# A dilated 3x3 convolution: two weight kinds of pairs 3 to 6 as 128-row matmuls over a doubled copy of the odd rows

## The chip, the cores and the metric

The kernel runs on one core of a Trainium2 chip. The metric is device time in microseconds (us) of one execution. Three runs of the kernel before gave 126.81, 126.86 and 127.06 us; the median is 126.86 us. One further execution was profiled; everything said about single instructions and transfers comes from that one.

Engines are named as in the profile: PE is TensorE (PEld is its loading of weights), DVE is VectorE, ACT is ScalarE, POOL is GpSimd, and SP is SyncE, whose queue issues all transfers of this kernel.

## The reference

A batch of 16 images with 64 channels of 64 x 64 is convolved to 128 channels with a 3 x 3 kernel of dilation 2 and zero padding, in float32:

```python
batch, c_in, h, w, c_out, k, dilation = 16, 64, 64, 64, 128, 3, 2
pad = dilated_k // 2                       # 2
for kh in range(k):
    for kw in range(k):
        output[b, co] += weight[co, ci, kh, kw] * x_pad[b, ci, kh*dilation:kh*dilation+h, kw*dilation:kw*dilation+w]
```

So an output row r needs the input rows r-2, r and r+2, each at three column shifts. 16.8 MB are read and 33.6 MB are written.

## The kernel before

**Layout.** Two images make a pair: the 64 channels of the one lie on partitions 0 to 63, those of the other on 64 to 127. There are 8 pairs (0 to 7), and each is cut into 4 groups of 16 output rows, so there are 32 groups G; `pb, g = divmod(G, 4)` gives the pair and the group in it.

**Arithmetic.** The rows are taken two by two. In each block of four rows, rows 0 and 1 are the even part E and rows 2 and 3 the odd part O. Dilation 2 means that the row above an even part is the odd part of the block before, and the row below it is the odd part of its own block. With w0, w1, w2 for the three kernel rows, the kernel forms E+O once and then

- even output = w1 (E+O) + (w2-w1) O + w0 O of the block before,
- odd output = w1 (E+O) + (w0-w1) E + w2 E of the block after.

The five products are called kinds 0 to 4: w1, w2-w1, w0, w0-w1, w2. `product` (line 182) makes one kind: for each of three column shifts j, and for each of the two images, one matmul that contracts over 64 partitions (the two halves of the array work on the two images) with up to 512 columns. `psP` (kind 0, 6 matmuls), `psA` (kinds 1 and 2, 12 matmuls, even output) and `psB` (kinds 3 and 4, 12 matmuls, odd output) are PSUM tiles of two banks; psP has one buffer, psA and psB share three.

**One group** (lines 219 to 263): PE makes psP, psA, psB in this order (in G = 0: psA, psB, psP). ACT copies psP to `p_sb` (L251), then does its casts. DVE makes the sum E+O of the next group (`rowsum`, L95), then adds psA + p_sb and psB + p_sb into the output ring `osb` (L258), a ring of three pairs.

**Casts.** x arrives as float32 (`x32`, three buffers) and is cast to float16 (`x16`, four buffers) in chunks of a group, at the places of the hand-written table `CASTS` (L162): ACT (L83) or POOL (L85). POOL has 7 of the 32 chunks, the last at G = 6.

**Transfers.** All are issued by SP in program order, which is the order of the one queue: the weights; pair 0 in two pieces, pairs 1 and 2; then, by the table `LOADS` (L215), pair 3 in G = 0, 4 in G = 2, 5 in G = 3, 6 in G = 7, 7 in G = 11. A load waits until the casts of the pair that had its buffer are done. A pair's output goes out when its last group is added (`pair_store`, two transfers of 2 MB); the first four rows of one image go out at G = 0. Pair 7 goes out in halves: at G = 29 one image's 32 rows (1 MB), the other's first 24 rows (768 KB) and its next `ROWS4` = 8 rows as two transfers, partitions 0 to 123 (248 KB) and 124 to 127 (8 KB); at G = 31 two transfers of 1 MB.

**Opening.** The weights are combined on DVE, POOL and ACT, turned by matmuls against an identity and copied into `w_sb`, duplicated on both halves of the partitions (lines 113 to 158).

Of the kernel before, what the change touches and what calls it, by code (L numbers as in the profile page):

```python
# [10 lines left out]
def kernel(  # L11
# [7 lines left out]
    nc = tc.nc  # L19

    B, CI, H, W = x.shape
    CO, CI_w, KH, KW = weight.shape
# [4 lines left out]
    d = 2  # L27

    P = 128
    f32 = mybir.dt.float32  # L30
    f16 = mybir.dt.float16
# [5 lines left out]
    NG = H // GR  # L37
    NBLK = GR // 4
    NH = GR // 2 * W
    npairs = B // 2  # L40
    ngroups = npairs * NG
# [3 lines left out]

    wpool = ctx.enter_context(tc.tile_pool(name="wpool", bufs=1))
    fpool = ctx.enter_context(tc.tile_pool(name="fpool", bufs=XF))
    xpool = ctx.enter_context(tc.tile_pool(name="xpool", bufs=4))
    sxpool = ctx.enter_context(tc.tile_pool(name="sxpool", bufs=2))
    opool = ctx.enter_context(tc.tile_pool(name="opool", bufs=1))  # L50
    spool = ctx.enter_context(tc.tile_pool(name="spool", bufs=3))
# [1 line left out]
    apool = ctx.enter_context(tc.tile_pool(name="apool", bufs=3, space=bass.MemoryType.PSUM))  # L53
# [6 lines left out]
    x32_tiles, x16_tiles, xs_tiles = {}, {}, {}  # L60

    def load(pb, cuts=(0, H)):
        x32_tiles[pb] = fpool.tile([P, HW], f32, tag="x32", name="x32")
        for lo, hi in zip(cuts[:-1], cuts[1:]):
            nc.sync.dma_start(
                out=x32_tiles[pb][:, lo * W : hi * W], in_=x_pair[pb, :, lo * W : hi * W]
            )
# [3 lines left out]
    def o_pair(pb):  # L71
        at = pb % OB * 2 * HW
        return o_ring[:, at : at + 2 * HW]

    def cast(c, eng):
        pb, g = divmod(c, NG)
        lo, hi = chunk_rows[g]
        if g == 0:
            x16_tiles[pb] = xpool.tile([P, HW], f16, tag="x16", name="x16")
        out = x16_tiles[pb][:, lo * W : hi * W]  # L80
        in_ = x32_tiles[pb][:, lo * W : hi * W]
        if eng is nc.scalar:
            eng.copy(out=out, in_=in_)  # L83
        else:
            eng.tensor_copy(out=out, in_=in_)  # L85

    def rowsum(c):
        pb, g = divmod(c, NG)
        if g == 0:
            xs_tiles[pb] = sxpool.tile([P, HW // 2], f16, tag="xs", name="xs")  # L90
        v = x16_tiles[pb][:, g * GR * W : (g + 1) * GR * W].rearrange(
            "p (b e q) -> p b e q", e=2, q=2 * W
        )
        s = xs_tiles[pb][:, g * NH : (g + 1) * NH].rearrange("p (b q) -> p b q", q=2 * W)
        nc.vector.tensor_tensor(out=s, in0=v[:, :, 0], in1=v[:, :, 1], op=add)  # L95

    w32 = wpool.tile([CO, CI * KH * KW], f32, name="w32")
    nc.sync.dma_start(out=w32, in_=weight.rearrange("o i h w -> o (i h w)"))
    load(0, (0, 2 * GR + d, H))
# [1 line left out]
    load(2)  # L101
    zero = wpool.tile([P, 512], f16, name="zero")
    nc.vector.memset(zero, 0.0)  # L103
    ident = wpool.tile([P, P], f16, name="ident")
    make_identity(nc, ident)

# [11 lines left out]
    w_sb = wpool.tile([P, NT * CO], f16, name="w_sb")  # L118
# [10 lines left out]
    def turn(k):  # L129
# [24 lines left out]
        out=x16_tiles[0][:, 8 * W : 18 * W], in_=x32_tiles[0][:, 8 * W : 18 * W]  # L154
# [5 lines left out]

    A, B_ = nc.scalar, nc.gpsimd
    CASTS = {  # L162
        0: ((1, A), (2, A), (3, B_)),
        1: ((4, A), (5, A), (6, B_)),
        2: ((7, A), (8, A), (9, B_)),
        3: ((10, A), (11, B_)),
        4: ((12, A), (13, A), (14, B_)),
        5: ((15, A), (16, B_)),
        6: ((17, A), (18, A), (19, B_)),
        8: ((20, A), (21, A)),  # L170
        9: ((22, A), (23, A)),
        19: ((24, A), (25, A)),
        20: ((26, A), (27, A)),
        24: ((28, A), (29, A)),
        25: ((30, A), (31, A)),
    }

    def casts(G):
        for c, eng in CASTS.get(G, ()):
            cast(c, eng)  # L180

    def product(ps, src, kind, blk0, nblk, first, last):
        for j in (1, 0, 2):
            dw = (j - 1) * d
            o0, o1 = max(0, -dw), W - max(0, dw)
            t = kind * KW + j
            for hb in range(2):
                pp = slice(hb * CI, (hb + 1) * CI)
                rhs = src(pp, dw + o0, dw + o1)
                po = ps[:, hb * NH + blk0 * 2 * W : hb * NH + (blk0 + nblk) * 2 * W]  # L190
                po = po.rearrange("p (r w) -> p r w", w=W)[:, :, o0:o1]
                nc.tensor.matmul(  # L192
                    out=po,
                    lhsT=w_sb[pp, t * CO : (t + 1) * CO],
                    rhs=rhs,
                    start=first and j == 1,
                    stop=last and j == 2,
                )

    def blocks(x16, b0, n, e):  # L200
        v = x16.rearrange("p (b e r w) -> p b e r w", e=2, r=2, w=W)
        return lambda pp, c0, c1: v[pp, b0 : b0 + n, e, :, c0:c1]

    def store(pb, m, r0=0, r1=H, rows=((0, P),)):
        for lo, hi in rows:
            nc.sync.dma_start(
                out=out_img[2 * pb + m, lo:hi, r0 * W : r1 * W],
                in_=o_pair(pb)[lo:hi, m * HW + r0 * W : m * HW + r1 * W],
            )

    def pair_store(pb):
        for m in range(2):
            store(pb, m, GR // 4 if pb == m == 0 else 0)

    LOADS = {0: (3,), 2: (4,), 3: (5,), 7: (6,), 11: (7,)}  # L215
    FOUR = ((0, P - 4), (P - 4, P))
    ROWS4 = 8

    for G in range(ngroups):
        pb, g = divmod(G, NG)  # L220
        x16 = x16_tiles[pb]
        xs = xs_tiles[pb].rearrange("p (r w) -> p r w", w=W)
        o = o_pair(pb).rearrange("p (m b e q) -> p m b e q", m=2, e=2, q=2 * W)
        b0 = g * NBLK

        def summed():
            ps = ppool.tile([P, 2 * NH], f32, tag="p", name="psP")
            sv = lambda pp, c0, c1: xs[pp, g * GR // 2 : (g + 1) * GR // 2, c0:c1]
            product(ps, sv, 0, 0, NBLK, True, True)
            return ps  # L230

        if G:
            psP = summed()

        psA = apool.tile([P, 2 * NH], f32, tag="ab", name="psA")
        product(psA, blocks(x16, b0, NBLK, 1), 1, 0, NBLK, True, False)
        z = 1 if g == 0 else 0
        product(psA, blocks(x16, b0 + z - 1, NBLK - z, 1), 2, z, NBLK - z, False, True)

        psB = apool.tile([P, 2 * NH], f32, tag="ab", name="psB")  # L240
        product(psB, blocks(x16, b0, NBLK, 0), 3, 0, NBLK, True, False)
        z = 1 if g == NG - 1 else 0
        product(psB, blocks(x16, b0 + 1, NBLK - z, 0), 4, 0, NBLK - z, False, True)

        if not G:
            psP = summed()

        if not G:
            casts(0)
        p_sb = spool.tile([P, 2 * NH], f32, tag="psb", name="p_sb")  # L250
        nc.scalar.copy(out=p_sb, in_=psP)  # L251
        if G:
            casts(G)
        if G + 1 < ngroups:
            rowsum(G + 1)
        pv = p_sb.rearrange("p (m b q) -> p m b q", m=2, q=2 * W)
        for e, ps in ((0, psA), (1, psB)):
            nc.vector.tensor_tensor(  # L258
                out=o[:, :, b0 : b0 + NBLK, e],
                in0=ps.rearrange("p (m b q) -> p m b q", m=2, q=2 * W),  # L260
                in1=pv,
                op=add,
            )

        later = pb in (1, 2)
        if g == NG - 1 and later:
            pair_store(pb)
        for q in LOADS.get(G, ()):
            load(q)
        if G == 0:  # L270
            store(0, 0, 0, GR // 4)
        if pb == npairs - 1:
            if g % 2 == 1:
                store(pb, 0, (g - 1) * GR, (g + 1) * GR)
                if g == 1:
                    store(pb, 1, 0, 2 * GR - ROWS4)
                    store(pb, 1, 2 * GR - ROWS4, 2 * GR, FOUR)
                else:
                    store(pb, 1, (g - 1) * GR, (g + 1) * GR)
        elif g == NG - 1 and not later:  # L280
            pair_store(pb)
# [35 lines left out]
```

## Time and profile before

| | |
|---|---|
| median of three runs | 126.86 us (126.81 to 127.06) |
| the profiled execution: its own time | 126.71 us |
| its span, first to last instruction | 124.9 us |
| PE busy | 104.9 us, 84% |
| DVE busy | 92.1 us, 74% |
| ACT busy | 58.7 us, 47% |
| POOL busy | 9.6 us, 8% |
| transfers | 50.78 MB, 405 GB/s of HBM traffic over the span |
| one psA or psB matmul of 64 x 496 | 369 ns from start to modelled end |
| one p_sb copy | 1012 ns |
| one add into osb | 1224 ns (psA), 1220 ns (psB) |
| one rowsum | 468 ns mean, 416 ns median |

A busy time is the union of an engine's instructions. The page's second part cuts the span into 40 slices (3.12 us each) and gives busy tenths; its chain of work starts at the instruction that ended last and goes back to what released each step. Matmuls overlap, so a matmul's 369 ns is longer than the step from one to the next. A transfer is spread over 16 DMA engines, and each engine reports by itself when its part has landed; the trace keeps these reports and each packet's start and length.

### The profile page before, as it was taken

Reading aid. Unit: us, or ns where it says so; the run is one execution under the profiler, and the core shown is the slowest. Engines: PE = TensorE matmul, PEld = TensorE weight load, DVE = VectorE, ACT = ScalarE, POOL = GpSimd, SP = SyncE. Lnnn points to the kernel's source line nnn. Section 1 sums busy time; section 2 is a strip of 40 time slices with the busy share of each in tenths; the row PEclk is TensorE's granted clock in tenths of the full one; section 3 lists DMA queues with packets and bytes.
Section 4 is the critical chain, followed back from the end, with each engine's and each line's share of the span. In section 5 each row is a group of like instructions: output and inputs, shape, how many; then the busy total and the mean of one; then the engine's idle time right before and its main releaser. Section 6 shows DMA issues by size and latency. Waiting matters only on the chain.

```text
span 124.9 us, 2345 instructions
## 1 busy us (share of the span) xinstructions
PE 104.9 (84%) x1000; PEld 55.7 (45%) x1000; DVE 92.1 (74%) x103; ACT 58.7 (47%) x61; POOL 9.6 (8%) x15
## 2 busy tenths in 40 slices
PE   6886998999999999999999999999999999700000
PEld 2343444555555555555555555555555555300000
DVE  0753997979998889888988898889888988720000
ACT  4375866698569533333333893339933333300000
POOL 2411306023300000000000000000000000000000
PEclk9999999999999999999999999999999999996555
DMA  4999999999999999999999999999999999999981
GB/s 120 385 439 435 441 430 435 404 430 430 333 433 424 420 441 435 422 420 425 435 420 435 435 428 425 420 435 420 430 441 430 425 420 430 430 407 420 430 378 60
DMA packets 4322, 50.78 MB, mean 406 GB/s; under 512 B 472, under 2 KB 600, under 8 KB 1112
## 3 DMA queue, kind: packets, MB, share of 16 engines
q1 hardware_dynamic: 4312, 50.63, 96.5%
q8 instruction: 8, 0.13, 0.4%
q14 instruction: 2, 0.02, 0.0%
HBM read 17.07 MB, written 33.55 MB: 405 GB/s over the span
## 4 chain that ended last, share of the span: by engine, by line
PE 69%; DVE 1%; DVEq 1%; issue 0%
PE psA L192 28%; PE psB L192 27%; PE psP L192 14%; DVE osb L258 1%; DVEq L312 1%; DVEq L258 0%
## 5 line engine op out<-in xcount | busy, mean ns | idle before, releaser
L192 PEld LDWEIGHTS <-w_sb 64*128 64x128 f16 x960 | 53.7, 94 | 48.1 <-issue 2.0
L251 ACT COPY p_sb<-psP 128x1024 f32<-128x1024 f32 x32 | 32.4, 1012 | 40.2 <-PE psP L192 39.2
L258 DVE TENSOR_TENSOR osb<-psA,p_sb 128x1024 f32<-128x1024 f32 x32 | 39.2, 1224 | 13.1 <-PE psA L192 7.8
L192 PE MATMUL psA<-x,w_sb 64*128 64x496 f16 (+3 forms) x384 | 45.0, 365 | 0.5 <-ACT x L156 0.5
L192 PE MATMUL psB<-x,w_sb 64*128 64x496 f16 (+3 forms) x384 | 45.0, 365 | 0.0
L258 DVE TENSOR_TENSOR osb<-psB,p_sb 128x1024 f32<-128x1024 f32 x32 | 39.0, 1220 | 0.0
L192 PE MATMUL psP<-xs,w_sb 64*128 64x496 f16 (+1 forms) x192 | 26.0, 371 | 1.7 <-ACT p_sb L251 1.5
L83 ACT CAST x<-x 128x1024 f16<-128x1024 f32 (+2 forms) x24 | 24.3, 1049 | 4.2 <-DMA x<-in_x_dram 4.0
L95 DVE TENSOR_TENSOR xs<-x 128x512 f16<-128x512 f16 x32 | 15.0, 468 | 0.7 <-ACT x L83 0.7
L85 POOL CAST x<-x 128x896 f16<-128x896 f32 (+2 forms) x7 | 7.4, 1068 | 19.7 <-DMA x<-in_x_dram 15.4
L111 PE MATMUL dm<-zero 128*128 128x512 f16 x10 | 4.1, 532 | 1.2 <-DVE zero L103 1.2
L121 DVE CAST wd<-w 128x192 f16<-128x192 f32 x1 | 0.5, 501 | 2.6 <-DMA w<-in_weight_dram 2.6
L111 PEld LDWEIGHTS <-zero 128*128 128x128 f16 x10 | 1.0, 121 | 2.6 <-DVE zero L103 1.2
L134 PEld LDWEIGHTS <-wd 128*64 128x64 f16 x30 | 1.0, 112 | 1.9 <-DVE wd L121 1.3
L134 PE MATMUL wt<-ident,wd 128*64 128x128 f16 x30 | 1.4, 226 | 0.3 <-DVE wd L121 0.3
L123 ACT ACT_TABLE_LOAD x1 | 1.3, 1283 | 0.7 <-PEq L298 0.7
L123 ACT CAST wd<-w 128x192 f16<-128x192 f32 x1 | 0.5, 541 | 1.7 <-DMA w<-in_weight_dram 1.7
L146 ACT CAST w_sb<-wt 128x384 f16<-128x384 f32 x1 | 0.5, 479 | 1.3 <-PE wt L134 1.3
L122 POOL TENSOR_TENSOR wd<-w 128x192 f16<-128x192 f32 x1 | 0.8, 797 | 2.5 <-DMA w<-in_weight_dram 2.5
L103 DVE MEMSET zero<- 128x256 uint32 x1 | 0.3, 272 | 0.9 <-PEq L298 0.9
L156 ACT CAST x<-x 128x512 f16<-128x512 f32 x1 | 0.6, 617 | 0.6 <-DMA x<-in_x_dram 0.6
L125 POOL CAST wd<-w 128x192 f16<-128x192 f32 x1 | 0.8, 812 | 0.0
(12 smaller groups left out, 4.3 us busy)
## 6 DMA issues: line engine op xcount, KB each, us to landing
out_dram<-osb SPq DMA_DIRECT2D x13, 2048.0 KB, 19.2
x<-in_x_dram SPq DMA_DIRECT2D x7, 2048.0 KB, 14.8
out_dram<-osb SPq DMA_DIRECT2D x3, 1024.0 KB, 13.6
out_dram<-osb SPq DMA_DIRECT2D x1, 1920.0 KB, 16.8
x<-in_x_dram SPq DMA_DIRECT2D x1, 1088.0 KB, 5.4
x<-in_x_dram SPq DMA_DIRECT2D x1, 960.0 KB, 7.2
out_dram<-osb SPq DMA_DIRECT2D x1, 768.0 KB, 15.0
w<-in_weight_dram SPq DMA_DIRECT2D x1, 288.0 KB, 3.0
```

Of the source, the lines that this page charges most:

```text
L83: eng.copy(out=out, in_=in_)
L85: eng.tensor_copy(out=out, in_=in_)
L95: nc.vector.tensor_tensor(out=s, in0=v[:, :, 0], in1=v[:, :, 1], op=add)
L111: nc.tensor.matmul(out=dm[:, 0:512], lhsT=zero[:, 0:P], rhs=zero)
L122: nc.gpsimd.tensor_tensor(out=wdv[:, 3], in0=wv[:, 0], in1=wv[:, 1], op=sub)
L123: nc.scalar.copy(out=wdv[:, 2], in_=wv[:, 0])
L125: nc.gpsimd.tensor_copy(out=wdv[:, 4], in_=wv[:, 2])
L134: nc.tensor.matmul(out=wts[k % 3][r * CI : (r + 1) * CI, c0 + j * CO : c0 + (j + 1) * CO], lhsT=wd[:, t * CI : (t + 1) * CI], rhs=ident,)
L192: nc.tensor.matmul(out=po, lhsT=w_sb[pp, t * CO : (t + 1) * CO], rhs=rhs, start=first and j == 1, stop=last and j == 2,)
L251: nc.scalar.copy(out=p_sb, in_=psP)
L258: nc.vector.tensor_tensor(out=o[:, :, b0 : b0 + NBLK, e], in0=ps.rearrange("p (m b q) -> p m b q", m=2, q=2 * W), in1=pv, op=add,)
L312: with _tile.TileContext(nc) as tc:
```

## The change

- **Doubled odd rows.** A ring `xo` of four slots (one for each g) holds, for each of the two images m, the odd rows of a group twice: O on the image's own 64 partitions and O of the block before on the other 64. `shift` fills it with four copies of 64 partitions x 512 float16 for a group, three on POOL and one on ACT, in group G for group G + 2, for the groups of pairs 3 to 6. In the first group of an image the copies of the block before leave out the first block, whose place stays zero from two memsets on POOL in the opening.
- **128-row matmuls.** For pairs 3 to 6 `stacked` replaces the two products of psA: six matmuls (three shifts, two images) contract over 128 partitions and make kinds 1 and 2 at once, with weights `w_st` that four POOL copies put together in the opening. psP and psB stay as they were, on 64 rows.
- **Order.** In pairs 3 to 6 an even group makes psP, psB, psA and an odd one psA, psP, psB, so that the 128-row matmuls of two groups lie side by side; DVE adds in the same order. G = 0 makes psA, psP, psB.
- **Casts.** From chunk 12 on there is one cast in each group, on ACT: chunk c in group c - 8 up to pair 5 and c - 6 for pairs 6 and 7. POOL loses chunks 14, 16 and 19. In G = 0 one of three casts goes ahead of the copy of psP, the other two behind it.
- **Sizes.** x16 has three buffers instead of four; `ROWS4` is 7 instead of 8, so that the transfer ahead has 25 rows.

```diff
-    xpool = ctx.enter_context(tc.tile_pool(name="xpool", bufs=4))
+    xpool = ctx.enter_context(tc.tile_pool(name="xpool", bufs=3))
...
+    xo_ring = wpool.tile([P, NG * 2 * NH], f16, name="xo")
+    xo = xo_ring.rearrange("p (g m n) -> p g m n", g=NG, m=2)
+
+    def shift(c, engines):
+        pb, g = divmod(c, NG)
+        v = x16_tiles[pb].rearrange("p (b e q) -> p b e q", e=2, q=2 * W)
+        it = iter(engines)
+        for m in range(2):
+            own = slice(m * CI, (m + 1) * CI)
+            for late in range(2):
+                lanes = own if not late else slice((1 - m) * CI, (2 - m) * CI)
+                z = 1 if late and g == 0 else 0
+                to = xo[lanes, g, m, z * 2 * W :].rearrange("p (b q) -> p b q", q=2 * W)
+                at = g * NBLK - late + z
+                src = v[own, at : at + NBLK - z, 1]
+                eng = next(it)
+                if eng is nc.scalar:
+                    eng.copy(out=to, in_=src)
+                else:
+                    eng.tensor_copy(out=to, in_=src)
...
+    nc.gpsimd.memset(xo[CI:P, 0, 0, 0 : 2 * W], 0.0)
+    nc.gpsimd.memset(xo[0:CI, 0, 1, 0 : 2 * W], 0.0)
...
-        0: ((1, A), (2, A), (3, B_)),
+        -1: ((1, A),),
+        0: ((2, A), (3, B_)),
...
-        4: ((12, A), (13, A), (14, B_)),
-        5: ((15, A), (16, B_)),
-        6: ((17, A), (18, A), (19, B_)),
-        8: ((20, A), (21, A)),
-        9: ((22, A), (23, A)),
-        19: ((24, A), (25, A)),
-        20: ((26, A), (27, A)),
-        24: ((28, A), (29, A)),
-        25: ((30, A), (31, A)),
     }
+    for c in range(3 * NG, ngroups):
+        CASTS[c - (8 if c < 6 * NG else 6)] = ((c, A),)
...
+    STACKED = range(3, 7)
+    w_st = wpool.tile([P, 2 * KW * CO], f16, name="w_st")
+    for m in range(2):
+        for r in range(2):
+            pp = slice(r * CI, (r + 1) * CI)
+            kind = 1 + (m + r) % 2
+            nc.gpsimd.tensor_copy(
+                out=w_st[pp, m * KW * CO : (m + 1) * KW * CO],
+                in_=w_sb[pp, kind * KW * CO : (kind + 1) * KW * CO],
+            )
+
+    def stacked(ps, g):
+        for j in (1, 0, 2):
+            dw = (j - 1) * d
+            o0, o1 = max(0, -dw), W - max(0, dw)
+            for m in range(2):
+                t = m * KW + j
+                rows = lambda v: v.rearrange("p (r w) -> p r w", w=W)
+                nc.tensor.matmul(
+                    out=rows(ps[:, m * NH : (m + 1) * NH])[:, :, o0:o1],
+                    lhsT=w_st[:, t * CO : (t + 1) * CO],
+                    rhs=rows(xo[:, g, m])[:, :, dw + o0 : dw + o1],
+                    start=j == 1,
+                    stop=j == 2,
+                )
...
-    ROWS4 = 8
+    ROWS4 = 7
...
+        late = pb in STACKED and g % 2 == 0
+        if G == 0:
+            psA, psP, psB = even(), summed(), odd()
+        elif late:
+            psP, psB, psA = summed(), odd(), even()
+        elif pb in STACKED:
+            psA, psP, psB = even(), summed(), odd()
+        else:
+            psP, psA, psB = summed(), even(), odd()
 
         if not G:
-            psP = summed()
-
-        if not G:
-            casts(0)
+            casts(-1)
         p_sb = spool.tile([P, 2 * NH], f32, tag="psb", name="p_sb")
         nc.scalar.copy(out=p_sb, in_=psP)
-        if G:
-            casts(G)
+        casts(G)
+        if (G + 2) // NG in STACKED:
+            shift(G + 2, (nc.gpsimd, nc.gpsimd, nc.scalar, nc.gpsimd))
         if G + 1 < ngroups:
             rowsum(G + 1)
         pv = p_sb.rearrange("p (m b q) -> p m b q", m=2, q=2 * W)
-        for e, ps in ((0, psA), (1, psB)):
+        for e, ps in ((1, psB), (0, psA)) if late else ((0, psA), (1, psB)):
```

`even` and `odd` are the lines that made psA and psB before, as functions; `even` calls `stacked` for pairs 3 to 6.

More of the change, by code (lines that the diff above doesn't have):

```diff
@@ L230, in summed, with even, odd @@
             return ps
-        if G:
-            psP = summed()
[L235 to L243, printed above, removed]
+        def even():
+            ps = apool.tile([P, 2 * NH], f32, tag="ab", name="psA")
+            if pb in STACKED:
+                stacked(ps, g)
+            else:
+                product(ps, blocks(x16, b0, NBLK, 1), 1, 0, NBLK, True, False)
+                z = 1 if g == 0 else 0
+                product(ps, blocks(x16, b0 + z - 1, NBLK - z, 1), 2, z, NBLK - z, False, True)
+            return ps
+        def odd():
+            ps = apool.tile([P, 2 * NH], f32, tag="ab", name="psB")
+            product(ps, blocks(x16, b0, NBLK, 0), 3, 0, NBLK, True, False)
+            z = 1 if g == NG - 1 else 0
+            product(ps, blocks(x16, b0 + 1, NBLK - z, 0), 4, 0, NBLK - z, False, True)
+            return ps
+        late = pb in STACKED and g % 2 == 0
[5 more added lines that the diff above has]
+            psA, psP, psB = even(), summed(), odd()
+        else:
+            psP, psA, psB = summed(), even(), odd()
         if not G:
-            psP = summed()
-        if not G:
-            casts(0)
+            casts(-1)
         p_sb = spool.tile([P, 2 * NH], f32, tag="psb", name="p_sb")
         nc.scalar.copy(out=p_sb, in_=psP)
-        if G:
-            casts(G)
+        casts(G)
+        if (G + 2) // NG in STACKED:
+            shift(G + 2, (nc.gpsimd, nc.gpsimd, nc.scalar, nc.gpsimd))
         if G + 1 < ngroups:
```

## The prediction

> **What bounds the kernel now.** I read the page's slices first, then the chain of work, then the windows, and last the transfers. The slices:
>
> ```profile
> PE   6886998999999999999999999999999999700000
> DMA  4999999999999999999999999999999999999981
> ```
>
> PE is full until slice 34 and then has nothing to do for five slices (15 us); the DMA engines are full from slice 1 to the last but one. The chain ends long before the span does:
>
> ```profile
> 106.25 1.28 PE psA L192 x12
> ...
> 107.62 1.23 DVE osb L258
> 108.85 1.13 DVEq L312
> ```
>
> Computing is over at about 110 us. The windows (busy time of PE, PEld, DVE, ACT, POOL, then clock, DMA share, GB/s) say what the rest is:
>
> ```profile
> 46.00:97.00 51.00, 51.00 (x500) 28.06 (x498) 45.40 (x50) 23.78 (x25) 0.00 (x0) 1.00 1.01 428
> 109.00:120.00 11.00, 0.00 (x0) 0.00 (x0) 0.98 (x1) 0.00 (x0) 0.00 (x0) 0.71 1.00 419
> 120.00:125.00 5.00, 0.00 (x0) 0.00 (x0) 0.00 (x0) 0.00 (x0) 0.00 (x0) 0.50 0.38 159
> ```
>
> So the bound is the transfers: 428 GB/s while PE works, 419 after it has stopped. The only idle DMA time is at the start and in the tail, of which this is a close view (117 to 125 us in slices of 0.2 us):
>
> ```profile
> DMA  9699999999999998995895652252220100000000
> ```
>
> The engines run dry one after another from about 120 us. The trace's list of landings (one for each engine and transfer) gives the last 1 MB store: the first engine is done at 120.58 us, the median at 122.15, the last at 124.04. **The time is the end of the latest DMA engine** plus 0.9 us to the span's end and 1.8 us around it (126.71 own time less 124.9 span). Which engine is that? Following the packets, one engine takes 633 to 662 ns for each 16 KB packet that it writes from 38 to 109 us, where the others take 611; it does not do so while loads 6 and 7 pass, nor after computing ends. In 92 such packets it loses about 92 x 33 ns = 3.0 us, and it is the one at 124.04. The next is at 123.93, and it is one of four (123.23, 123.32, 123.45, 123.93) that carry the transfers cut by ROWS4: the 248 KB transfer landed on four engines only, 31 packets of 2 KB each, and the 8 KB one put one more on each.
>
> **The change part by part.**
>
> *PE.* The 128-row matmuls save no PE time. In the opening two 128-row matmuls of 512 columns follow each other by 0.21 us; the chain has 12 of the 64-row ones in 1.27 us, which is 0.21 us for each two, one on each half. Six at 0.21 us are 1.27 us again. In the first group of an image psA took 1.11 us, since it left out the missing block; the new one runs over zeros, +0.16 us x 4 groups = 0.64 us. Each pair of groups enters and leaves the 128-row form once: 16 switches. The trace has one place that shows such a switch undisturbed, and one with other causes in it:
>
> ```profile
> 5.58 0.10 PEld L111 LDWEIGHTS <-zero 128*128 128x128 f16 x1
> 5.90 0.36 PEld L134 LDWEIGHTS <-wd 128*64 128x64 f16 x12 [0.23 <-issue]
> 6.36 0.10 PEld L111 LDWEIGHTS <-zero 128*128 128x128 f16 x1
> 7.19 0.17 PEld L192 LDWEIGHTS <-w_sb 64*128 64x128 f16 x4 [0.74 <-PE dm L111]
> ```
>
> The third row is nothing, the second 0.23 us, the fourth (which waits for x as well) 0.74. I take 0.23, the row without another cause: 16 x 0.23 = 3.7 us, with the ends 0 and 11.8. Computing ends 4.3 us later, at 113 instead of 108.85 us. The Trainium skill's TensorEngine Tiling (Key Properties) says that changing the tiling mode drains TensorE; it gives no price, and by it the sum stands at the 3.7 us just taken instead of at nothing.
>
> *Is that hidden?* Stores wait in a full queue. SP issued pair 6's stores at 97.64 us, but the transfer ahead of them landed at 101.6 (first engine) to 104.9 (latest one); the last two stores were issued at 110.0 and the engines came to them at 115.7 to 119.2. A transfer moves about 1 us after its issue (weights issued at 0.73, first data at 1.74). So the latest engine has 6.2 us to spare at pair 6 and 8 us at the end. The engines that come first have about 3 us at pair 6, and as they also finish 2 to 3 us early, a gap of theirs costs nothing. All of the 4.3 us are covered; without this cover they would be 4.3 us of time.
>
> *POOL and DVE.* Three copies of 512 columns a group. POOL's casts took 1043 ns for 1024 columns and 934 for 896, 0.85 ns a column over a start of 0.17, so 0.61 us each and 1.8 us of a group's 3.17. What they touch is the rowsum:
>
> ```profile
> 13.77 1.04 POOL L85 CAST x<-x 128x1024 f16<-128x1024 f32 x1 [3.93 <-DMA x<-in_x_dram]
> 13.79 1.29 DVE L95 TENSOR_TENSOR xs<-x 128x512 f16<-128x512 f16 x1
> 30.09 0.42 DVE L95 TENSOR_TENSOR xs<-x 128x512 f16<-128x512 f16 x1
> ```
>
> A rowsum that starts in a POOL instruction waits until that one is over (at 13.79), and takes 0.42 us otherwise; the adds into osb keep 1.22 us beside POOL. At most 0.61 us a group is added. DVE's steps are 0.33 + 1.13 + 1.13 = 2.6 us of 3.17, so it reaches 3.2 at the worst: 16 x 0.03 = 0.5 us, covered as above.
>
> *ACT.* One p_sb copy (0.91 us from start to start), one cast (0.95) and one copy of 512 columns (at most the 0.62 us of the cast of 512 columns at 6.58 us): 2.5 us of 3.17. In pairs 3 to 6 the odd group's psP is followed by the next psP after 1.27 us, just the 1.2 us that the copy out of its single buffer takes; if it is late by 0.1 us, 8 such places cost 0.8 us, covered too.
>
> *Loads.* Loads 6 and 7 stand on SP behind the stores of pairs 1 and 2 (issued 36.99 and 49.30 us). They need casts 15 and 19, now in G = 7 and 11, done by about 34 and 47 us, so nothing moves. Load 7 landed at 75.05 us and its first cast is in G = 22, at about 79 us; load 6 at 60.45, with its first cast at 67. Three x16 buffers suffice: chunk 12 in G = 4 needs pair 0, whose last matmuls come before psP of G = 4.
>
> *Opening.* With psP in the middle, p_sb of G = 0 is about 1.2 us earlier; but then ACT waits for pair 1, which landed at 13.7 us, and for pair 2 at 19.7, so the gain is gone by G = 3. The four POOL copies (about 0.5 us each, from 6.3 us on) end before POOL's cast at 8.9. The queue is full meanwhile: nothing.
>
> *ROWS4.* Packets of 2048 B start every 80 ns, those of 8192 B every 305. Going to 7 rows adds 256 B to eight packets on each engine, 2 KB at 27 B/ns = **+0.08 us on all sixteen**, and takes 32 x 256 B = 8 KB, 0.30 us, from the four: **-0.23 us on these**. The Trainium skill, DMA: Bandwidth & Descriptors (Why a DMA increments its semaphore by 16 and not by 1), has the rule: the largest number of engines up to 16 that divides the rows, the lowest-numbered ones. For 124 that is four; the four landings agree.
>
> *The slow engine.* It loses 33 ns a packet only while instructions run. A group had 60 PE instructions, 3 on DVE and 2 on ACT; now 48, 3, 3 and 3 on POOL: 57 for 65, 12% fewer. If its loss follows the number of instructions, it saves 12% of 33 ns in the some 63 packets that it writes in these groups: -0.25 us. The bounds are 0 (it depends on something else) and the whole of those packets' loss, -2.1 us. I take -0.25, since the loss stops when the instructions stop.
>
> *Sum.* Latest engine 124.04 - 0.25 + 0.08 = 123.87; the four 123.93 - 0.23 = 123.70. The end moves by -0.17 us: 126.54 against the profiled 126.71, and against the median, 0.15 above that, **126.7 us**.
>
> **Rivals.**
>
> *A. Slow in itself.* The engine's loss has nothing to do with instructions; the time is 126.86 + 0.08 = 126.94. For it: the loss is steady through stages with more and with less ACT work. Against: it ends with computing. The Trainium skill, DMA: Bandwidth & Descriptors (Latency and other measured facts), says that engines 7 and 15 are usually slower than the rest; by that the sum is this rival's, and the trace agrees so far that one engine is.
>
> *B. The latest engine is relieved more.* PE's program is fetched in packets of 16 KB, eight in this run, each about 0.95 us on one engine; 192 instructions fewer make that six or seven. If the loss falls by half or a fetch leaves a late engine, the four at 123.70 set the end: -0.34, 126.5 us; if one of theirs goes too, 126.1.
>
> *C. The switch is dear.* At 0.74 us, 16 switches and 0.64 make computing end 12.5 us later, at 121.4; the last stores go out at 122.5, move 1 us later, take 4.9 us and end at 128.4 instead of 124.0: 131.2 us. It decides from (8 - 0.64)/16 = 0.46 us a switch.
>
> *D. It does not do what it says*: one fetch or packet more falls on the latest engine, from ACT's and POOL's longer programs, +0.3 to +0.95: 127.2 to 127.8.
>
> **How the numbers follow.** Forecast 0.42 (126.45 to 126.95), A 0.22, B 0.20, C 0.11, D 0.05. The three runs lie 0.25 us apart, so 0.2% is what can be told from no change: below 126.61 is B and a quarter of the forecast, 0.31; above 127.11 C, D and a little of A, 0.18; between, 0.51. The range runs from B's lower end, 126.1, to D, 127.6; C's far end is left out.
>
> **What would show it.** Six 128-row matmuls in 1.27 us, gaps of about 0.2 us at 16 switches, PE ending near 112 us, rowsums of 0.4 to 1.0 us, the DMA row full all the same, a tail of the same length. It is wrong if the DMA row shows holes before 110 us (the cover is gone), or if the last landing moves by more than 0.4 us.

## The result, and the profile after

The changed kernel takes **128.26 us** (median of six runs, 128.06 to 128.88) against 126.85 us of the kernel before on the same chip: a ratio of 1.0114, with a 95% interval of 1.0099 to 1.0128. It is 1.4 us slower, and the forecast of 126.7 us with its range of 126.1 to 127.6 us was wrong. The profiled execution took 128.27 us, with a span of 126.5 us. The slices of the changed kernel:

```profile
PE   6999994999999999999999999999999999940000
DMA  4999999999999999999999999999999979999991
```

The DMA row looks as before but for one 7, in slice 32 (101 to 104 us). The chain's end says how late computing is:

```profile
109.79 1.28 PE psA L211 x12
...
111.17 1.23 DVE osb L315
112.39 1.13 DVEq L369
```

The last add begins 3.55 us later than before, a little less than the 4.3 us that the prediction reckoned. So the compute side is about as late as forecast, and it is the cover of this lateness by the transfers that has to be looked at. SP's queue gives the moment at which pair 6's stores go out, in the kernel before and in the changed one:

```profile
97.64 1.03 SPq L206 DMA_DIRECT2D out_dram<-osb  x2
```

```profile
101.99 0.82 SPq L251 DMA_DIRECT2D out_dram<-osb  x2
```

They go out 4.35 us later. The transfers seen closely, 99 to 109 us in slices of 0.25 us, before and after:

```profile
DMA  9699699999999799997977999799796997969969
```

```profile
DMA  6799979996734309099090990909919094390919
```

There is a **hole** around 102.5 us, and behind it the digits alternate between 9 and 0. Each digit sums the time of the packets that begin in its slice (so a share can pass 1.00). A packet of 16 KB takes 611 ns, over two slices; engines that work at different phases fill every slice about equally. Alternation means that nearly all sixteen begin their packets at the same time. The landings say the same: of pair 6's first store, fourteen engines land between 108.13 and 108.36 us (before, the first fourteen were spread from 106.51 to 108.26). The engines that had been ahead have waited for the others; **they stand level**.

The windows of the two kernels (busy time of PE, PEld, DVE, ACT, POOL, then clock, DMA share, GB/s), before:

```profile
101.00:104.00 3.00, 3.00 (x32) 1.62 (x30) 2.72 (x3) 0.84 (x1) 0.00 (x0) 1.00 1.02 437
117.00:120.00 3.00, 0.00 (x0) 0.00 (x0) 0.00 (x0) 0.00 (x0) 0.00 (x0) 0.50 1.03 432
```

and after:

```profile
101.00:104.00 3.00, 3.00 (x34) 1.70 (x31) 3.00 (x4) 1.00 (x2) 0.00 (x0) 1.00 0.70 295
117.00:120.00 3.00, 0.00 (x0) 0.00 (x0) 0.00 (x0) 0.00 (x0) 0.00 (x0) 0.50 1.02 328
```

The first line is the hole: a DMA share of 0.70. The second is something else: the engines are busy all the time (1.02) and yet move 328 GB/s instead of 432. In these 3 us the small rows of pair 7 pass on four engines; the packets of 8 KB beside them take up to 958 ns; before, all of them took 309. The close view of the tail (8 us from 118.6, slices of 0.2 us) ends 1.6 us later than before:

```profile
DMA  9669599898999999999984422311301100000000
```

The last four landings, 124.91, 125.19, 125.34 and 125.60 us, are those of the four engines that carry the small rows; of the other twelve the last lands at 124.15.

What the change put on the engines, from the page's groups:

```profile
L118 POOL COPY xo<-x 64x512 f16<-64x512 f16 (+1 forms) x48 | 29.1, 607 | 36.3 <-PE psA L237 27.4
L237 PE MATMUL psA<-xo,w_st 128*128 128x496 f16 (+1 forms) x96 | 21.7, 376 | 0.0
L116 ACT COPY xo<-x 64x512 f16<-64x512 f16 x16 | 9.8, 615 | 0.3
```

A POOL copy takes 607 ns, as reckoned (0.61 us), and one on ACT 615.

### The profile page after: what moved, and what is told of

Same layout as the page of the kernel before. It is cut to its first block, busy times and chain, and to the rows that moved or that the text cites. A ratio compares the mean times of both kernels' runs of the same rounds, so it can differ in the third digit from the quotient of the medians.

```text
span 126.5 us, 2239 instructions
## 1 busy us (share of the span) xinstructions
PE 108.4 (86%) x904; PEld 52.3 (41%) x904; DVE 91.3 (72%) x103; ACT 72.5 (57%) x80; POOL 38.1 (30%) x66
## 2 busy tenths in 40 slices
DMA packets 4322, 50.77 MB, mean 401 GB/s; under 512 B 472, under 2 KB 728, under 8 KB 1112
## 3 DMA queue, kind: packets, MB, share of 16 engines
q1 hardware_dynamic: 4312, 50.63, 95.9%
## 4 chain that ended last, share of the span: by engine, by line
PE 70%; DVE 1%; DVEq 1%; issue 0%
PE psB L211 26%; PE psA L237 17%; PE psP L211 16%; PE psA L211 12%; DVE osb L315 1%; DVEq L369 1%; DVEq L315 0%
## 5 line engine op out<-in xcount | busy, mean ns | idle before, releaser
L211 PEld LDWEIGHTS <-w_sb 64*128 64x128 f16 x768 | 41.5, 94 | 42.3 <-issue 7.3
L118 POOL COPY xo<-x 64x512 f16<-64x512 f16 (+1 forms) x48 | 29.1, 607 | 36.3 <-PE psA L237 27.4
L83 ACT CAST x<-x 128x1024 f16<-128x1024 f32 (+2 forms) x27 | 28.2, 1050 | 4.9 <-DMA x<-in_x_dram 4.6
L211 PE MATMUL psA<-x,w_sb 64*128 64x496 f16 (+2 forms) x192 | 22.5, 365 | 0.3 <-ACT x L181 0.3
L237 PE MATMUL psA<-xo,w_st 128*128 128x496 f16 (+1 forms) x96 | 21.7, 376 | 0.0
L237 PEld LDWEIGHTS <-w_st 128*128 128x128 f16 x96 | 8.7, 98 | 12.4 <-issue 2.9
L116 ACT COPY xo<-x 64x512 f16<-64x512 f16 x16 | 9.8, 615 | 0.3
L85 POOL CAST x<-x 128x896 f16<-128x896 f32 (+1 forms) x4 | 3.9, 993 | 8.9 <-DMA x<-in_x_dram 8.8
L225 POOL COPY w_st<-w_sb 64x384 f16<-64x384 f16 x4 | 2.4, 607 | 1.3 <-ACT w_sb L171 1.2
```

The costliest lines, as they stand in the source:

```text
L116: eng.copy(out=to, in_=src)
L118: eng.tensor_copy(out=to, in_=src)
L211: nc.tensor.matmul(out=po, lhsT=w_sb[pp, t * CO : (t + 1) * CO], rhs=rhs, start=first and j == 1, stop=last and j == 2,)
L225: nc.gpsimd.tensor_copy(out=w_st[pp, m * KW * CO : (m + 1) * KW * CO], in_=w_sb[pp, kind * KW * CO : (kind + 1) * KW * CO],)
L237: nc.tensor.matmul(out=rows(ps[:, m * NH : (m + 1) * NH])[:, :, o0:o1], lhsT=w_st[:, t * CO : (t + 1) * CO], rhs=rows(xo[:, g, m])[:, :, d ...
```

## The experiments

Two theories stood against each other at first. **H**: late compute lets the transfer queue run dry at pair 6's stores; the hole lines the engines up; the four engines that carry the small rows lose the lead that made room for that load, and end the span. **P**: the 1792-byte packets of the 7 small rows make the writes slow. Others came up on the way (each stacked pair costs by itself; the copies on POOL and ACT; late compute as such). Each ratio is to the kernel before, run on the same chip at the same time (medians of 126.76 to 126.88 us); it is not the ratio of the two medians, so the two can differ a little.

**b_rows7.** In the kernel before:

```diff
-    ROWS4 = 8
+    ROWS4 = 7
```

> The kernel before with 7 small rows instead of 8, nothing else. Theory H (a hole in the transfers at pair 6's stores lines the DMA engines up, and the four engines that carry the small rows then end last): there is no hole here, so only the sum of the prediction applies, +0.08 us, 126.9 us. Rival P (the 1792-byte packets that begin at byte 6400 of a row slow down all writes while they pass, as the after kernel's windows from 117 to 120 us suggest with 336, 274 and 375 GB/s): the loss shows here too, 127.4 to 127.8 us, and the last 1 MB stores land 3.3 us behind the transfer ahead instead of 2.45.

Measured: 126.95 us, ratio 1.0028 (1.0002 to 1.0055); 430 GB/s from 117 to 120 us. P falls: the same packets pass at full rate here. The profiled execution itself (127.52 us) was not a typical one of this kernel.

**a_rows8.** In the kernel after:

```diff
-    ROWS4 = 7
+    ROWS4 = 8
```

> The kernel after with 8 small rows instead of 7, nothing else. Theory H: the hole stays, the four engines carry 0.23 us more, 128.3 to 128.6 us. Rival P: the writes between 117 and 120 us run at full rate again, 0.7 us less, 127.4 to 127.7 us.

Measured: 128.76 us, ratio 1.0164 (1.0145 to 1.0184). Slower than with 7 rows, as H has it, but by 0.50 us where 0.23 were expected, and so above its 128.3 to 128.6; 322 GB/s from 117 to 120 us, so the slow writes do not need 1792-byte packets.

**a_nosplit.** In the kernel after:

```diff
-                    store(pb, 1, 0, 2 * GR - ROWS4)
-                    store(pb, 1, 2 * GR - ROWS4, 2 * GR, FOUR)
+                    store(pb, 1, 0, 2 * GR)
```

> The kernel after with the small rows not split off: that store goes out as one 1 MB transfer over all sixteen engines. Theory H: the four engines lose their 1.6 us of extra load, and the latest of the other engines ends the span (119.3 at the transfer ahead, plus 0.6, plus 4.9): 124.8 instead of 125.6 us for the last landing, 127.2 to 127.6 us of time. If the four engines have nothing to do with it, 128.3 us or more.

Measured: 127.57 us, ratio 1.0073 (1.0051 to 1.0094). Its windows, with the hole still there, though a smaller one in this execution:

```profile
101.00:104.00 3.00, 3.00 (x33) 1.64 (x31) 3.00 (x4) 1.00 (x2) 0.00 (x0) 1.00 0.85 360
117.00:120.00 3.00, 0.00 (x0) 0.00 (x0) 0.00 (x0) 0.00 (x0) 0.00 (x0) 0.50 1.03 434
```

Without the split the writes run at 434 GB/s behind a hole, too. The last landing is at 124.76 us, on an engine that is late from before the hole (104.82 us at the transfer ahead of pair 6's stores).

**b_delay.** In the kernel before, ahead of the sums in `summed`:

```diff
+            for _ in range((2 if g == 0 else 1) if pb in range(3, 7) else 0):
+                for hb in range(2):
+                    pp = slice(hb * CI, (hb + 1) * CI)
+                    nc.tensor.matmul(
+                        out=ps[:, hb * NH : (hb + 1) * NH].rearrange("p (r w) -> p r w", w=W),
+                        lhsT=w_sb[pp, CO : 2 * CO],
+                        rhs=sv(pp, 0, W),
+                        start=True,
+                        stop=True,
+                    )
             product(ps, sv, 0, 0, NBLK, True, True)
```

> The kernel before with redundant matmuls ahead of the sums in pairs 3 to 6 (their result is overwritten): 20 times 0.21 us, so that PE is 4.2 us later at the end of pair 6, with the old order, no doubled rows, no 128-row matmuls, no extra work on POOL and ACT, and 8 small rows. Theory H: pair 6's stores are issued at about 101.9 us instead of 97.6, the same hole opens, and the time is 127.4 to 128.2 us. If the extra time comes from POOL's and ACT's copies or from the 128-row matmuls beside the transfers, it stays at 126.9 us.

Measured: 128.83 us, ratio 1.0166 (1.0151 to 1.0182), the number of the kernel after with 8 small rows. The stores of pair 6 go out at 102.25 us, and the windows are those of the changed kernel:

```profile
101.00:104.00 3.00, 3.00 (x34) 1.44 (x32) 2.84 (x5) 1.01 (x1) 0.00 (x0) 1.00 0.70 295
117.00:120.00 3.00, 0.00 (x0) 0.00 (x0) 0.00 (x0) 0.00 (x0) 0.00 (x0) 0.63 1.03 343
```

So late matmuls alone, with nothing else of the change, make the hole, the level engines, the slow writes and the time. It came out higher than I expected (127.4 to 128.2): I had not counted the slow writes, which show here as 343 GB/s.

**a_three_pairs.** In the kernel after:

```diff
-    STACKED = range(3, 7)
+    STACKED = range(3, 6)
```

> The kernel after with the 128-row matmuls in pairs 3 to 5 only; pair 6 is as in the kernel before. Theory H: PE is 2.6 us late at pair 6 instead of 3.3, and the adds of its last group no longer come late, so the stores go out near 100.2 us (after: 102.0), the engines that are free at 101.6 find work, they keep their lead, and the time is 126.8 to 127.2 us, though three of the four stacked pairs are there. If each stacked pair costs time by itself, three quarters of the loss stay: 127.8 to 128.0 us.

Measured: 126.93 us, ratio 1.0005 (0.9994 to 1.0016). Pair 6's stores go out at 100.42 us, and from 101 to 104 us 426 GB/s are moved. Three of four stacked pairs cost nothing that can be measured; with the fourth, the stores go out 1.57 us later and the whole loss is there.

**a_pair6_halves.** In the kernel after:

```diff
+        elif pb == npairs - 2:
+            if g % 2 == 1:
+                for m in range(2):
+                    store(pb, m, (g - 1) * GR, (g + 1) * GR)
         elif g == NG - 1 and not later:
             pair_store(pb)
```

> The kernel after with all its compute, PE as late as there, but pair 6 is stored in halves (four transfers of 1 MB, two after its second group, two after its last). Theory H: the first half goes out near 96 us, ahead of the moment at which the queue runs dry, so there is no hole, the four engines keep their lead, and the slow writes between 117 and 120 us are gone too: 126.6 to 127.1 us. If late compute by itself costs the time, 128.2 us.

Measured: 126.94 us, ratio 1.0009 (0.9995 to 1.0024). All of the compute is as late as in the changed kernel, but the first half of pair 6 goes out at 95.4 us, and the loss is gone, the slow writes with it:

```profile
101.00:104.00 3.00, 3.00 (x34) 1.70 (x32) 3.00 (x4) 1.00 (x2) 0.00 (x0) 1.00 0.94 399
117.00:120.00 3.00, 0.00 (x0) 0.00 (x0) 0.00 (x0) 0.00 (x0) 0.00 (x0) 0.50 1.03 429
```

**a_order27.** In the kernel after:

```diff
-        elif pb in STACKED:
+        elif pb in STACKED and G != 27:
             psA, psP, psB = even(), summed(), odd()
```

> The kernel after with group 27 alone, the last of pair 6, in the old order (psP, psA, psB): two switches more, but psP is copied about 2.5 us earlier, so that the two adds do not both come behind it. Theory H with the order as a part of it: pair 6's stores go out 0.8 to 1.0 us earlier (101.1 instead of 102.0), the hole shrinks by as much, and the time falls by 0.5 to 0.9 us, to 127.4 to 127.8 us. If the order costs nothing: 128.2 us.

Measured: 127.49 us, ratio 1.0055 (1.0031 to 1.0078). The stores go out at 101.24 us, 0.75 us earlier, and the time falls by 0.77 us. The order of the products in one group is a good half of the loss.

**b_spare_engine.** In the kernel before, an attempt to relieve the slow engine:

```diff
-    ROWS4 = 8
+    ROWS4 = 6
...
-                    store(pb, 1, 0, 2 * GR - ROWS4)
+                    store(pb, 1, 0, 2 * GR - ROWS4, ((0, P - 8), (P - 8, P)))
```

> The kernel before with pair 7's large store at G = 29 cut into partitions 0 to 119 and 120 to 127, and 6 small rows instead of 8. By the number of rows 120 goes over fifteen engines and 8 over eight. If the engine that is slow is the sixteenth, it is relieved by eight packets of 6.6 KB, about 2.0 us, and the four engines by 0.5 us, while eight engines get one packet more: the last landing falls from 124.0 to about 123.6 us, 126.2 to 126.6 us of time. If the slow engine is one of the first eight, it gets more instead: 127.0 to 127.4 us.

Measured: 129.63 us, ratio 1.0214 (1.0171 to 1.0258), slower than both of my expectations. The store of 120 partitions reported from fifteen engines and that of 8 from eight, as the expectation has it, but from 117 to 120 us only 339 GB/s were moved, without any hole. Uneven transfers again made the writes slow, and this hides whether the slow engine is the sixteenth: that stays open.

**a_sixteen.** In the kernel after:

```diff
-                    store(pb, 1, 2 * GR - ROWS4, 2 * GR, FOUR)
+                    store(pb, 1, 2 * GR - ROWS4, 2 * GR)
```

> The kernel after with its 7 small rows as one transfer of 128 partitions, so that the same 1792-byte packets go over all sixteen engines and not four. Theory H: the hole stays and lines the engines up; without the load on four of them the result is that of the unsplit store, 127.4 to 127.7 us, and the writes between 117 and 120 us run at over 410 GB/s, so that the slow writes belong to the four-engine transfer. If they belong to the small packets, these stretches stay below 380 GB/s and the time is over 128 us.

Measured: 127.68 us, ratio 1.0094 (1.0054 to 1.0134); of the ten runs eight lie between 127.51 and 127.96 us and two at 129.21 and 129.44. With the same hole, the same level engines and the same packet size, the rate is

```profile
101.00:104.00 3.00, 3.00 (x34) 1.70 (x32) 3.00 (x4) 1.00 (x2) 0.00 (x0) 1.00 0.70 295
117.00:120.00 3.00, 0.00 (x0) 0.00 (x0) 0.00 (x0) 0.00 (x0) 0.00 (x0) 0.51 1.02 423
```

423 instead of 328 GB/s: behind a hole, it is the transfer over four engines that slows the writes.

**b_delay_half.** As b_delay, with:

```diff
-            for _ in range((2 if g == 0 else 1) if pb in range(3, 7) else 0):
+            for _ in range((2 if g == 0 else 1) if pb in range(3, 5) else 0):
```

> The kernel before with the redundant matmuls in pairs 3 and 4 only: PE is 2.1 us late from pair 5 on instead of 4.2. Theory H has a threshold: pair 6's stores go out near 99.7 us and their data moves from about 101.0, just before the first engine runs dry at 101.6, so nothing is lost: 126.7 to 127.1 us. If late PE costs time in proportion, half of 2.0 us is lost: 127.8 us.

Measured: 127.19 us, ratio 1.0020 (0.9999 to 1.0042), between the two expectations and nearer to the threshold. The profiled execution is a late one (127.78 us; its first psA began at 8.44 us, in the kernel before at 7.25): its stores went out at 100.85 us, not 99.7, with a small hole (410 GB/s from 101 to 104 us). The proportional loss of 1.0 us is excluded.

**a_opening.** In the kernel after:

```diff
-    STACKED = range(3, 7)
+    STACKED = range(0)
...
-    ROWS4 = 7
+    ROWS4 = 8
```

> The kernel after with no stacked pair and no copies, and 8 small rows: what is left of the change is the order of G = 0, the casts one a group, the three x16 buffers, and the setup of the weights on POOL. The prediction put all of this at nothing: 126.7 to 127.0 us. If the later loads or casts cost something, over 127.2 us.

Measured: 126.84 us, ratio 0.9991 (0.9969 to 1.0014). The opening, the casts and the three x16 buffers cost and bring nothing.

**a_copies.** In the kernel after, in `even`:

```diff
-            if pb in STACKED:
-                stacked(ps, g)
-            else:
+            if True:
```

> The kernel after with its copies on POOL and ACT, its order of products and its adds, but psA made by the 64-row matmuls as before, so that nothing reads the doubled rows. It leaves out the switches and the multiplications by zero, about 2.3 us of PE by the chain of work. Theory H: pair 6's stores go out at about 99.6 us (1.0 us of it from the order of the adds), before the queue runs dry: 126.7 to 127.1 us. If the copies or the order cost the time by themselves: 128 us.

Measured: 126.91 us, ratio 1.0006 (0.9985 to 1.0027); stores at 99.85 us. The copies and the order alone stay below the point from which time is lost.

**b_nosplit.** The edit of a_nosplit in the kernel before.

> The kernel before with the 8 small rows not split off, one 1 MB transfer over all sixteen engines. Theory H: the latest engine gets its share of eight packets again, +0.64 us, 127.4 to 127.5 us. Then late compute costs only 0.1 to 0.2 us where nothing is split (127.57 measured with it), and nearly all of its 1.4 us in the changed kernel is the meeting of the hole with the split. If the hole costs time by itself, this kernel is at 126.8 us and the hole's share is 0.7 us.

Measured: 127.59 us, ratio 1.0058 (1.0039 to 1.0077), a little above the 127.4 to 127.5 expected. That completes a table of medians:

| | small rows on four engines | not split off |
|---|---|---|
| compute in time (before) | 126.85 | 127.59 |
| compute late (after) | 128.26 | 127.57 |

The split kernels of the table have 8 small rows before and 7 after. With 7 in both (b_rows7) they take 126.95 and 128.26 us, with 8 in both (a_rows8) 126.85 and 128.76. Where nothing is split, the hole costs nothing that can be measured. With the split it costs 1.3 us at 7 rows and 1.9 at 8, and all of that is its meeting with the four-engine transfer: splitting gains 0.7 us when the four engines are ahead, and when they are not it loses 0.7 us with 7 rows and 1.2 with 8.

**a_cross.** In the kernel after:

```diff
-    FOUR = ((0, P - 4), (P - 4, P))
+    FOUR = ((0, P - 32), (P - 32, P))
```

> The kernel after with its 7 small rows cut at partition 96 instead of 124: 96 rows and 32 rows both go over sixteen engines, six and two packets on each, so the load is even, as in one transfer, but most packets come from other partitions than those the engine otherwise reads. If crossing partitions makes the writes slow: below 400 GB/s from 117 to 120 us, and over 127.9 us. If the concentration on four engines does it: over 415 GB/s and the 127.5 to 127.8 us of the uncut transfer.

Measured: 127.45 us, ratio 1.0050 (1.0031 to 1.0069), a little below the span expected of the even spread; 393 GB/s from 117 to 120 us, between the two expectations. Reading other partitions costs a little rate there and nothing at the end (last landing 124.77 us, as in a_sixteen). The concentration on four engines is the main part, as far as this one pair of runs can tell; by what mechanism it holds up the other twelve is not shown.

## Why the prediction was wrong, point by point

- **What bounds the kernel**: right. With compute up to 3.5 us later, a_three_pairs, a_pair6_halves and a_copies take the time of the kernel before.
- **The step that failed** is in the paragraph on what hides the late compute: "The engines that come first have about 3 us at pair 6, and as they also finish 2 to 3 us early, a gap of theirs costs nothing." Four of the early engines do not finish early. At the transfer ahead of the small rows they stood at 115.70, 115.84, 115.98 and 116.46 us, among the first seven; with the small rows they ended at 123.23 to 123.93, with the last. The prediction had both facts, and took their lead for spare time when it was already spent. In the changed kernel these four are level with the rest at 117.4 us, 1.4 us later on average, and end at 124.91 to 125.60.
- **What the small rows cost**: the same four needed 2.5 us for them before and 2.9 us after, though each packet is an eighth smaller; the sum had -0.30 us for it. This was in no rival.
- **PE**: reckoned 4.3 us late (16 switches at 0.23 us and 0.64), measured 3.4 us at the end of pair 6 (psP of G = 28 at 99.63 us, before 96.26). Pair 6 in the chain of the kernel before, from its first psP to that of the next pair:

```profile
83.89 0.64 PE psP L192 x6
...
96.26 0.64 PE psP L192 x6
```

  The same pair in the chain of the changed kernel:

```profile
86.40 0.81 PE psP L211 x6
87.22 1.27 PE psB L211 x12
88.48 2.64 PE psA L237 x12
91.13 0.74 PE psP L211 x6
91.87 1.27 PE psB L211 x12
93.13 0.69 PE psP L211 x6
93.83 1.27 PE psB L211 x12
95.09 2.64 PE psA L237 x12
97.74 0.74 PE psP L211 x6
98.48 1.11 PE psB L211 x12
99.59 0.04 issue
99.63 0.81 PE psP L211 x6
```

  and that of a_copies, with the same order and 64-row matmuls, at its ends and at two places:

```profile
84.85 0.81 PE psP L211 x6
...
86.93 2.38 PE psA L211 x24
89.31 0.63 PE psP L211 x6
...
93.17 2.54 PE psA L211 x24
95.70 0.64 PE psP L211 x6
...
97.48 0.81 PE psP L211 x6
```

  A pair takes 13.23 us (86.40 to 99.63), in a_copies 12.63, before 12.37. So 0.26 us is the order (psP waits for its one buffer, the psP of 0.69 and 0.81 us): 1.0 us in four pairs, where the prediction allowed up to 0.8. The other 0.60 us is the 128-row form: 0.16 for the zeros, as reckoned, and 0.44 for four switches, **0.11 us each**, half of the row that I took. They show as 2.64 for 2.54 us on the way in and 0.74 for 0.64 on the way out; without its switch, six 128-row matmuls take the 1.27 us reckoned. The Trainium skill's TensorEngine Tiling (Key Properties) calls a switch a drain; the trace agrees that it costs time, and this is its price here. The row of 0.23 us was not a switch of this kind: its weights, `wd 128*64`, have 128 rows like `zero 128*128` ahead of them, and only the columns change. The fourth row of that list, `w_sb 64*128`, is the one that goes from 128 to 64 rows.
- **The adds**: not reckoned, 1.0 us. PE is 3.4 us late at the end of pair 6, and its stores are 4.35. In an odd stacked group psA is ready long before psP is copied, and both adds queue behind that copy:

```profile
98.56 1.01 ACT L307 COPY p_sb<-psP 128x1024 f32<-128x1024 f32 x1 [2.97 <-issue]
99.61 1.23 DVE L315 TENSOR_TENSOR osb<-psA,p_sb 128x1024 f32<-128x1024 f32 x1 [1.29 <-ACT p_sb L307]
...
100.75 1.22 DVE L315 TENSOR_TENSOR osb<-psB,p_sb 128x1024 f32<-128x1024 f32 x1
```

  Before, in the last group of pair 6, the first of them ran while PE made psB (95.15 to 96.26 us):

```profile
95.25 1.22 DVE L258 TENSOR_TENSOR osb<-psA,p_sb 128x1024 f32<-128x1024 f32 x1 [0.42 <-PE psA L192]
96.39 1.21 DVE L258 TENSOR_TENSOR osb<-psB,p_sb 128x1024 f32<-128x1024 f32 x1
```

  a_order27 takes this away in the one group that counts and gets 0.77 us back. That the stores go out 4.35 us late, so near the 4.3 us reckoned, is luck: the switches were put too dear by 1.9 us, the order and the adds were left out of the 4.3.
- **POOL and DVE**: right. A copy is 607 ns, and beside the copies a rowsum takes between 0.41 and 0.78 us.
- **Loads, opening, casts, buffers**: right (a_opening).
- **The slow engine**: the term of -0.25 us was wrong. Between 46 and 101 us its packets took 644 ns on average in both kernels, with 12% fewer instructions in the second: its loss does not follow their number, which was rival A's point. Of the twelve engines without small rows the last landed at 124.15 us, near the 124.12 that A's +0.08 us gives. It did not set the end, so this decided nothing. The entry of the Trainium skill, DMA: Bandwidth & Descriptors (Latency and other measured facts), that A names ties its guess at the cause to software-made descriptors; here 4312 of the 4322 packets are on a hardware queue, and which of the sixteen engines is slow was not found, so it lends A little.
- **The rivals**: C had the right side and place (late compute uses up its cover) but the wrong point; it asked for 8 us of delay, by the latest engine and the end of the kernel, where 4.35 us at pair 6 were enough. B's fetch fewer came (seven of PE's program instead of eight), and D puts its cost on the latest engine; neither set the end. "It is wrong if the DMA row shows holes before 110 us" is what came, and the last landing moved by 1.56 us.

No version here beats the kernel before: a_three_pairs, a_pair6_halves, a_copies and a_opening are the same within their intervals.

## What to carry to other kernels

Where transfers bound a kernel, read the slack of compute at each store, engine by engine, from the first that runs dry and not only from the last. A gap in the early engines can be free, as it was here where nothing was split (127.59 and 127.57 us), or cost over 1 us, as it did where four of them had more to carry later. An engine's lead at one place may be spent at another by a transfer made to balance the end, so follow each engine to the last landing before calling its gap free. Where a store waits for the last of several adds, an order of products that delays the first operand of all of them delays the store, here by 0.75 us in one group.

## What the hardware showed that I had not expected

- After a gap the engines stay level: fourteen of sixteen landed within 0.23 us of each other 6 us after the hole, and thirteen within 0.12 us 5 us later (113.01 to 113.13 us).
- A transfer on four engines can slow the other twelve: 328 GB/s with it and 423 with the same rows on sixteen. With the engines spread (before) it did not: 432. Cut for fifteen engines, a store did it without a hole (339 GB/s, 129.63 us). The Trainium skill, DMA: Bandwidth & Descriptors (Why a DMA increments its semaphore by 16 and not by 1), gives the number of engines, and the landings agree with it for 124, 120 and 8 rows (four, fifteen and eight engines).
